# Weight loads of the first expert pairs issued at other points, and the last tile's row store in two halves

## The chip, the cores and the metric

The kernel runs on one core of a Trainium2 chip. The metric is the device time of one execution in microseconds (us). TensorE (PE) multiplies matrices, VectorE (DVE), ScalarE (ACT) and GpSimd (POOL) work elementwise, and SyncE (SP) does little but issue DMA transfers. Each engine takes its instructions strictly in the order in which they stand in the program, and waits on semaphores where they depend on another engine or on a transfer.

## The reference

One transformer layer over 1024 tokens of width 1024: a hybrid mixer (two kinds of gated linear attention, chunks of 16), a layer norm, and a mixture of experts with 64 experts of which each token takes two, then a second layer norm. What matters here is the second half:

```python
x = layer_norm(ALPHA * x + hybrid_mixer(x, ...), ln1_g, ln1_b)
# hierarchical_moe: the best of 8 groups, then the best two of its 8 experts, with gates
h = jax.nn.silu(xb_ @ w_gate[e]) * (xb_ @ w_up[e])     # per expert: 1024 -> 512
y = h @ w_down[e]                                      # 512 -> 1024, added to each token by its gate
x = layer_norm(ALPHA * x + y, ln2_g, ln2_b)
```

All 64 experts have three float32 matrices of 2 MB each, 384 MB in all, which are read once.

## The kernel before

**Stages.** Up to about 400 us the mixer runs. From there to about 535 us the output projection, the first norm and the router run over eight tiles of 128 tokens; each tile's normed rows go to the DRAM tensor `x1d` (`scaled_rows`, a store issued by ACT), and the router's counts become tables that say which tokens each expert gets. From about 535 us on the experts run in 32 pairs; a pair does two experts at once, each with up to 64 tokens in one half of the array. The first rows come from `x1d` by gathers (indirect DMAs that POOL issues by index tables); from pair 2 on PE picks a pair's rows out of a group of four pairs' rows (`picked`).

**Weights.** A weight matrix is a *unit* of 2 MB. Pair p owns units 6p to 6p+5: two gate matrices, two up matrices, two down matrices. PE multiplies all gate rows of a pair (`rows_by(p, 0, ...)`), then all up rows (`rows_by(p, 2, ...)`), then, after ACT's silu, DVE's product `sg` (silu(gate) times up), four PE transposes and DVE's copy `hT`, the down rows (`down`). Units wait in *rooms*: four `w1u`, four `w2u`, and for some early units two `w3u` rooms and a room in an old tile `VO1`. `load_unit(i)` issues unit i's load on SP's queue; `load_after(i)` issues the load that takes the room of unit i, after the product that read unit i. So the loads stand in one line on SP, and each waits until PE has freed its room. Units 4 to 10 are loaded during the router's last tiles: unit 9 in two halves, where the second half and unit 5 wait until the first gather has landed. Unit 11 takes the room of unit 0, unit 12 that of unit 1, 13 that of 2, 17 and 18 those of 8 and 9, 21 that of 12, 36 and 37 those of 28 and 29 (pair 4's down matrices), 38 and 39 those of 30 and 31 (pair 5's gate matrices).

**Order.** PE's order is the written one (`manual_schedule`). On the other engines a scheduler orders the instructions by its own estimate of when each can start, within the dependences; `after` and `order` in the code add further ones. In pair 4 DVE also spreads the second norm's vectors over partitions (`spread_out_rows`, a STREAM_SHUFFLE for each), applies the first norm's gain to gathered rows (`gained`) and finishes the first group's output rows (`finish_rows`).

Of the kernel before, what the change touches and what calls it, by code (L numbers as in the profile page):

```python
# [10 lines left out]
F32 = mybir.dt.float32  # L11
# [10 lines left out]
NT = T // 128  # L22
KT = D // 128
# [7 lines left out]
NOV = 80  # L31
# [28 lines left out]
def mixer_moe_kernel(ctx: ExitStack, tc: tile.TileContext, x_in, xT_in, wf_in, wv_in, wvg_in, wa2_in,  # L60
# [767 lines left out]
    sp2 = b1.enter_context(tc.tile_pool(name="sp2", bufs=2, reuse_waits="tile"))  # L828
    wr = rp.tile([128, KT, 72], F32, name="wr", bufs=1)
    S.dma_start(wr, wr_in)  # L830
    w1p = ctx.enter_context(tc.tile_pool(name="w1", bufs=W1N, side="right", reuse_waits="tile"))

    preR = tc.alloc_tile_pool(name="preR", bufs=1, side="right", reuse_waits="tile")
    rows = preR.tile([128, 4, 2, 512], F32, name="w3u")
# [5 lines left out]
    NU = 6 * npair  # L840
    utile = {}

    def load_unit(i):

        if i >= NU:
            return None
        src, e = units[i]
        shape = [128, 4, D] if src is wd_in else [128, KT, FF]
        r = i if i < 4 else (i - 2) if i < 10 else (i - 3 - (i > 19)) % (W1N + W2N)
        pool, name = ((preR if i == 4 else preL, "w3u") if i in (4, 5) else (voap, "VO1") if i in (10, 19) else  # L850
                      (w1p, "w1u") if r < W1N else (w2p, "w2u"))
        t = pool.tile(shape, F32, name=name)
        sv = src[e].rearrange("(p c) n -> p c n", c=4 if src is wd_in else KT)
        utile[i] = t
        if i == 9:
            pend.append((t[:, KT // 2:], sv[:, KT // 2:]))
            return nc.sync.dma_start(t[:, 0:KT // 2], sv[:, 0:KT // 2])
        if i < NU - NSPL:
            return nc.sync.dma_start(t, sv)
        if i % 2 == 0:  # L860
            pend.append((t, sv))
            return None
        cuts = (0, 1, 2, 3) if i == NU - 1 else (0, 4, 6, KT) if i == NU - 3 else (0, 2, 4) if src is wd_in else (0, 4, KT)
        both = pend[-1], (t, sv)
        for a_, b_ in zip(cuts, cuts[1:]):
            for t_, s_ in both:
                d = nc.sync.dma_start(t_[:, a_:b_], s_[:, a_:b_])
        for n in range(2) if i == NU - 1 else ():
            for t_, s_ in both:
                ns = slice(n * 512, (n + 1) * 512)  # L870
                d = nc.sync.dma_start(t_[:, 3, ns], s_[:, 3, ns])
        return d

    def load_after(i):

        if i not in (4, 5, 19):
            load_unit(i + W1N + W2N + (3 if i < 4 else 1 if i < 19 else 0))

    pend = []
    NSPL = 12  # L880
# [8 lines left out]
    def router(t):  # L889

        lt = lgt.pop(t)
        el = lt[:, 8:72].rearrange("p (g e) -> p g e", g=8)
        tl = lambda n, w, d=F32: sp2.tile([128, w], d, name=n)
        gm, gi = tl("gm", 8), tl("gi", 8, mybir.dt.uint32)
        V.max(gm, lt[:, 0:8])
        V.max_index(gi, gm, lt[:, 0:8])

        og = tl("og", 8)
        V.tensor_tensor(og, cst[:, C_I8:C_I8 + 8], gi[:, 0:1].to_broadcast([128, 8]), OP.not_equal)
        sel = sp2.tile([128, 8, 8], F32, name="sel")  # L900
        V.scalar_tensor_tensor(sel, og[:, :, None].to_broadcast([128, 8, 8]), -3e38, el, op0=OP.mult, op1=OP.add)
        sl = sel.rearrange("p g e -> p (g e)")
        em, ei = tl("em", 8), tl("ei", 8, mybir.dt.uint32)
        V.max(em, sl)
        V.max_index(ei, em, sl)
        rtop[t] = V.tensor_tensor(oh12[:, :, t], expert[:, None, :].to_broadcast([128, 2, NE]),
                                  ei[:, 0:2, None].to_broadcast([128, 2, NE]), OP.is_equal)
        m = sp2.tile([128, NE], BF, name="m", bufs=3)
        msb = sp2.tile([128, NE], BF, name="msb", bufs=3)
        V.tensor_copy(msb, msum)  # L910
        mop = V.tensor_tensor(m, oh1[:, t], oh2[:, t], OP.add)
        count = lambda: V.tensor_tensor(msum, msum, m, OP.add)

        fin = tl("fin", 1)
        order(V.tensor_tensor(fin, ei[:, 1:2], ei[:, 0:1], OP.is_gt), mop, "the ranks' product goes first")
        enc = sp2.tile([128, 2], F32, name="enc", bufs=3)
        V.scalar_tensor_tensor(enc, big2, fin, cst[:, C_TOK:C_I8].rearrange("p (a t) -> p a t", a=2)[:, :, t],
                               op0=OP.mult, op1=OP.add)
        mt[t] = m, msb, enc

        def gates(behind=None):

            gs = tl("gs", 8)
            gz = tl("gz", 1)
            ops = []
            V.tensor_scalar(gs, lt[:, 0:8], gm[:, 0:1], None, op0=OP.subtract)
            S.activation(gs, gs, AF.Exp, accum_out=gz)
            e2 = tl("e2", 1)
            S.activation(e2, em[:, 0:1], AF.Exp, bias=em[:, 1:2], scale=-1.0)
            gd = tl("gd", 1)  # L930
            ops.append(V.scalar_tensor_tensor(gd, e2, 1.0, gz, op0=OP.add, op1=OP.mult))
            V.reciprocal(gatev[:, t, 0:1], gd)
            V.tensor_tensor(gatev[:, t, 1:2], gatev[:, t, 0:1], e2, OP.mult)
            ops.append(count())
            if behind:
                for o in ops:
                    order(o, behind, "the rows that are to be fetched go first")

        if t < NT - 1:
            gates()  # L940
            return None
        return gates
# [105 lines left out]
    def scaled_rows(t):  # L1048

        r = rt[t]  # L1050
        rs, nm, _ = stats[t]
        for n in range(2):
            S.activation(r[:, n], r[:, n], AF.Identity, bias=nm, scale=rs)
        S.dma_start(x1d[t * 128:(t + 1) * 128].rearrange("p (a n) -> p a n", a=2), r)

    def logits(t):

# [386 lines left out]

    ys, outs, sums, ends, trow, grow = {}, [], {}, {}, [], []
    first = gather(xgs[2], sidx[:, 0:1])
    G.memset(one1, 1.0)
    G.memset(xgs[1], 0.0)
    for ld in (load_unit(5), nc.sync.dma_start(*pend.pop())):
        after(ld, first, "the rows of the first pair go before weights that are needed later")  # L1450

    def load_vectors():

# [15 lines left out]
    def pairs():  # L1469
# [4 lines left out]
        def rows_by(p, u, dst, xt, between={}):  # L1474
            for c in range(KT):
                for b in range(2):
                    PE.matmul(dst[64 * b:64 * b + 64], xt[:, c, 64 * b:64 * b + 64], utile[6 * p + u + b][:, c],  # L1477
                              start=(c == 0), stop=(c == KT - 1))
                if c in between:
                    between[c]()  # L1480
            for b in range(2):
                load_after(6 * p + u + b)

        def gate(p, gp):
            sg = mw.tile([128, FF], F32, name="sg", bufs=1)
# [16 lines left out]
        gather(xgs[0], sidx[:, 1:2])  # L1502
        fetch_rows(0, (1,))
        gp = ps_g.tile([128, FF], F32, name="gu")
        rows_by(0, 0, gp, xt)
        sg, _ = gate(0, gp)
        xt1 = transposed(xgs[0], xgs[2])
        up = ps_g.tile([128, FF], F32, name="gu")
# [141 lines left out]


    def block_tables():
        bt = w1p.tile([128, 4096], F32, name="w1u")
        at = [0]

        def t1(w):
# [115 lines left out]

    nfl = nc.values_load(over[0:1, 0:1], min_val=0, max_val=1, skip_runtime_bounds_check_because="a maximum of compares")  # L1773
    with tc.For_i(0, nfl):
        ovt = w1p.tile([128, 4, NOV], F32, name="w1u")
        ogate, oyid, oxid, oexp = ovt[:, 0], ovt[:, 1].bitcast(I32), ovt[:, 2].bitcast(I32), ovt[:, 3].bitcast(I32)
        block_tables()
        nblk = nc.values_load(onum[0:1, 0:1], min_val=0, max_val=NOV,
# [61 lines left out]
```

## Time and profile before

| | us |
|---|---|
| median of three runs | 1483.46 (1483.22 to 1483.67) |
| the profiled execution, its own time | 1484.21 |
| its span in the profile | 1482.4 |
| PE busy in the span | 1405.7 (95%) |
| DVE / ACT / POOL busy | 604.5 / 483.6 / 229.3 |
| bytes moved by DMA | 445.62 MB, mean 301 GB/s |

Each row of a timeline is a start, a duration, an engine, a source line, an operation with what it writes and reads, and in square brackets the engine's idle time before it and what ended it. Equal rows in sequence are merged (x2). "SPq" and "ACTq" are the queues of SP and ACT where a DMA is issued; a row of the DMA view gives the issues in a stretch of time, the size of one and the median time from issue to landing. The windows view gives for a stretch its length, the busy time of PE, PE's weight loads, DVE, ACT and POOL (number of instructions in brackets), the granted PE clock, the busy share of the 16 DMA engines and GB/s.

### The profile page before, as it was taken

To read this page: it belongs to the slowest core of one execution; us is meant where nothing else is said; L and a number is where in the kernel's file an instruction comes from. 1 tells how busy PE (TensorE), PEld (TensorE's weight loads), DVE (VectorE), ACT (ScalarE), POOL (GpSimd) and SP (SyncE) were. 2 spreads that over 40 slices of the span, in tenths; PEclk is the share of its full clock that TensorE was granted. 3 is DMA by queue.
4 is the path that set the end of the run, shared out by engine and by line. 5 is a ranking of instruction groups with operands and counts; after the bars stand their busy time and mean duration, and the time that the engine had idled before them with its cause. 6 is when DMAs were issued, how large, how long until landed. Compare 5 with 4: busy or idle time off the path is not lost. (4 is left out here: it accounts for less than half of the span.)

```text
span 1482.4 us, 25290 instructions
## 1 busy us (share of the span) xinstructions
PE 1405.7 (95%) x10651; PEld 822.1 (55%) x10651; DVE 604.5 (41%) x1465; ACT 483.6 (33%) x973; POOL 229.3 (15%) x165
## 2 busy tenths in 40 slices
PE   8999999999999989999998999998999998999996
PEld 7989889898888854344343344343433333433432
DVE  7577674867545843162141123133123013212313
ACT  6475555474413433312222211321222221221120
POOL 0000001010012212342402210130130130131000
PEclk9999999999999999999999999999999999999999
DMA  6110010101384479999999999999999999999995
GB/s 215 30 44 30 31 44 30 46 30 31 107 339 172 171 305 411 418 414 425 427 427 426 427 427 424 428 427 427 425 428 427 426 426 428 425 428 427 423 420 208
DMA packets 52944, 445.62 MB, mean 301 GB/s; under 512 B 9577, under 2 KB 10857, under 8 KB 27349
## 3 DMA queue, kind: packets, MB, share of 16 engines
q1 hardware_dynamic: 46344, 430.09, 70.2%
q0 software_dynamic: 4896, 8.84, 1.6%
q10 hardware_dynamic: 1584, 5.01, 0.9%
q8 instruction: 85, 1.39, 0.4%
q14 instruction: 35, 0.28, 0.1%
HBM read 440.33 MB, written 12.60 MB: 306 GB/s over the span
## 5 line engine op out<-in xcount | busy, mean ns | idle before, releaser
L1477 PE MATMUL gu<-w1u,VO 128*64 128x512 f32 x1040 | 252.5, 609 | 24.6 <-DMA w1u<-in_wu_dram 20.6
L1477 PE MATMUL gu<-w2u,VO 128*64 128x512 f32 x960 | 236.3, 607 | 23.0 <-DMA w2u<-in_wu_dram 22.7
L1230 ACT ACTIVATE VO<-tp,cols 128x128 f32<-128x128 f32 x256 | 96.1, 457 | 308.7 <-PE tp L1242 300.3
L1602 DVE TENSOR_TENSOR sg<-sg,gu 128x512 f32<-128x512 f32 x30 | 20.6, 688 | 420.3 <-PE gu L1477 420.3
L1477 PEld LDWEIGHTS gu<-w1u,VO 128*64 128x64 f32 x1040 | 80.0, 140 | 184.8 <-issue 142.7
L1477 PEld LDWEIGHTS gu<-w2u,VO 128*64 128x64 f32 x960 | 80.2, 140 | 167.6 <-issue 130.9
L1466 PE MATMUL gu<-w1u,hT 128*64 128x512 f32 x496 | 117.1, 598 | 2.0 <-issue 1.8
L176 PE MATMUL pp<-xh,wl 128*128 128x512 f32 x288 | 113.1, 393 | 0.0
L176 PE MATMUL pp<-xl,wh 128*128 128x512 f32 x288 | 113.0, 392 | 0.0
L176 PE MATMUL pp<-xh,wh 128*128 128x512 f32 x288 | 113.0, 392 | 0.0
L1466 PE MATMUL gu<-w2u,hT 128*64 128x512 f32 x480 | 109.5, 598 | 0.0
L1281 DVE SCALAR_TENSOR_TENSOR y<-gu,gcol,y 128x512 fp32r<-128x512 f32 x60 | 44.8, 749 | 141.1 <-ACT y L1280 141.0
L1242 PEld LDWEIGHTS <-parts 128*128 128x128 bf16 x1248 | 69.9, 98 | 46.9 <-issue 46.8
L1280 ACT ACTIVATE y<-gu,gcol 128x512 fp32r<-128x512 f32 x60 | 41.1, 686 | 158.3 <-PE gu L1466 157.9
L1486 ACT ACTIVATE sg<-gu 128x512 f32<-128x512 f32 x31 | 18.5, 597 | 188.9 <-PE gu L1477 188.9
L1242 PE MATMUL tp<-pick,parts 128*128 128x128 bf16 x1248 | 80.1, 220 | 0.0
L1466 PEld LDWEIGHTS gu<-w1u,hT 128*64 128x64 f32 x496 | 35.5, 136 | 59.8 <-issue 55.4
L1466 PEld LDWEIGHTS gu<-w2u,hT 128*64 128x64 f32 x480 | 32.7, 136 | 62.3 <-issue 61.5
L176 PEld LDWEIGHTS pp<-xh,wl 128*128 128x128 f32 x288 | 54.1, 188 | 11.5 <-issue 0.5
L176 PEld LDWEIGHTS pp<-xl,wh 128*128 128x128 f32 x288 | 54.1, 188 | 11.2 <-issue 0.2
L176 PEld LDWEIGHTS pp<-xh,wh 128*128 128x128 f32 x288 | 54.1, 188 | 11.0
L1395 POOL TENSOR_TENSOR rest<-VO,parts 128x1024 f32<-128x1024 f32 x11 | 29.7, 2698 | 194.2 <-ACT parts L1392 129.9
(401 smaller groups left out, 2209.2 us busy)
## 6 DMA issues: line engine op xcount, KB each, us to landing
w1u<-in_wg_dram SPq DMA_DIRECT2D x30, 2048.0 KB, 27.8
w2u<-in_wu_dram SPq DMA_DIRECT2D x30, 2048.0 KB, 27.9
w1u<-in_wu_dram SPq DMA_DIRECT2D x29, 2048.0 KB, 29.9
w2u<-in_wg_dram SPq DMA_DIRECT2D x29, 2048.0 KB, 25.8
w1u<-in_wd_dram SPq DMA_DIRECT2D x29, 2048.0 KB, 29.9
w2u<-in_wd_dram SPq DMA_DIRECT2D x28, 2048.0 KB, 29.0
wr<-in_wf_dram SPq DMA_DIRECT2D x36, 256.0 KB, 2.7
w1u<-in_wu_dram SPq DMA_DIRECT2D x6, 1024.0 KB, 23.5
```

What stands on the lines that cost most here:

```text
L176: PE.matmul(ps, w[:, k], x_[:, k, ts], start=(k == j == 0), stop=(k == KT - 1 and j == 2))
L1230: S.activation(xt[:, c], tp[:, i], AF.Identity, bias=cols[:, 42 + c:43 + c], scale=cols[:, 34 + c:35 + c])
L1242: PE.matmul(o, part[:, c], m, start=(i == 0), stop=(i == len(ms) - 1))
L1280: S.mul(yh[:, ns], yps[n], gate_col)
L1281: return V.scalar_tensor_tensor(yl[:, ns], yps[n], gate_col, yh[:, ns], op0=OP.mult, op1=OP.subtract)
L1395: first = E.tensor_tensor(rest, x, b0, OP.subtract)
L1466: PE.matmul(yps[n][64 * b:64 * b + 64], hT[:, c, 64 * b:64 * b + 64], utile[6 * p + 4 + b][:, c, n * 512:(n + 1) * 512], start=(c == 0), s ...
L1477: PE.matmul(dst[64 * b:64 * b + 64], xt[:, c, 64 * b:64 * b + 64], utile[6 * p + u + b][:, c], start=(c == 0), stop=(c == KT - 1))
L1486: return sg, S.activation(sg, gp, AF.Silu)
L1602: V.tensor_tensor(sg, sg, up, OP.mult)
```

## The change

1. Unit 9 loads whole where its first half was issued.
2. Unit 5 waits for a small POOL instruction (`one1`'s memset) that now stands behind the first gather's issue, not for the gather's landing.
3. Units 11 and 12 write into the tiles of units 0 and 1 themselves (a reshaped view, so that dependences are kept by parts of the tile) and load in two halves each: the first half after half of pair 0's gate product, the second at its end. For that the four `w1u` rooms become four tiles of their own names.
4. The last token tile's rows are stored to `x1d` in two halves, each after its own ACT pass.
5. The last tile's small cast `msb` (128x64) moves from DVE to ACT.

```diff
-    w1p = ctx.enter_context(tc.tile_pool(name="w1", bufs=W1N, side="right", reuse_waits="tile"))
+    w1p = ctx.enter_context(tc.tile_pool(name="w1", bufs=1, side="right", reuse_waits="tile"))
...
-    def load_unit(i):
+    def load_unit(i, half=None):
...
-                      (w1p, "w1u") if r < W1N else (w2p, "w2u"))
-        t = pool.tile(shape, F32, name=name)
-        sv = src[e].rearrange("(p c) n -> p c n", c=4 if src is wd_in else KT)
+                      (w1p, f"w1u{r}") if r < W1N else (w2p, "w2u"))
+        n = shape[1]
+        if i in (11, 12):
+            t = utile[i - 11].rearrange("p a b -> p (a b)").rearrange("p (a b) -> p a b", a=n)
+        else:
+            t = pool.tile(shape, F32, name=name)
+        sv = src[e].rearrange("(p c) n -> p c n", c=n)
+        if half is not None:
+            utile[i] = t
+            cs = slice(half * n // 2, (half + 1) * n // 2)
+            return nc.sync.dma_start(t[:, cs], sv[:, cs])
         utile[i] = t
-        if i == 9:
-            pend.append((t[:, KT // 2:], sv[:, KT // 2:]))
-            return nc.sync.dma_start(t[:, 0:KT // 2], sv[:, 0:KT // 2])
...
-        V.tensor_copy(msb, msum)
+        (S.copy if t == NT - 1 else V.tensor_copy)(msb, msum)
...
+        dst = x1d[t * 128:(t + 1) * 128].rearrange("p (a n) -> p a n", a=2)
         for n in range(2):
             S.activation(r[:, n], r[:, n], AF.Identity, bias=nm, scale=rs)
-        S.dma_start(x1d[t * 128:(t + 1) * 128].rearrange("p (a n) -> p a n", a=2), r)
+            if t == NT - 1:
+                S.dma_start(dst[:, n], r[:, n])
+        if t < NT - 1:
+            S.dma_start(dst, r)
...
     first = gather(xgs[2], sidx[:, 0:1])
-    G.memset(one1, 1.0)
+    issued = G.memset(one1, 1.0)
     G.memset(xgs[1], 0.0)
-    for ld in (load_unit(5), nc.sync.dma_start(*pend.pop())):
-        after(ld, first, "the rows of the first pair go before weights that are needed later")
+    order(issued, first, "the rows of the first pair go before weights that are needed later")
+    after(load_unit(5), issued, "the rows of the first pair go before weights that are needed later")
...
             for b in range(2):
-                load_after(6 * p + u + b)
+                load_after(6 * p + u + b, None if p or u else 1)
...
-        rows_by(0, 0, gp, xt)
+        rows_by(0, 0, gp, xt, {KT // 2 - 1: lambda: [load_after(b, 0) for b in range(2)]})
```

**SP's loads around the first gather.** The rows are units 8, 9 (first half), 5, 9 (second half), 11, 12, 13 before, and 8, 9, 5, then the halves of 11 and 12, and 13 with the change. DMASW0 is the first gather's landing; PE is a wait for a room.

```order
L859 DMA w2u_6557<-in_wu_dram 128x4096 [waits PE_49]
L857 DMA w2u_6559<-in_wu_dram 128x2048 [waits DVE_49,PE_49]
L859 DMA w3u_6684<-in_wd_dram 128x4096 [waits DVE_49,DMASW0_49,PE_49,DMAHW0_49,Activation_49,Pool_49]
L1449 DMA w2u_6559<-in_wu_dram 128x2048 [waits DMAHW1_49]
L859 DMA w1u_6745<-in_wd_dram 128x4096 [waits DMAHW2_49,PE_49]
L859 DMA w1u_6747<-in_wg_dram 128x4096 [waits DMAHW3_49,PE_49]
L859 DMA w1u_6797<-in_wg_dram 128x4096 [waits DMAHW4_49,PE_49]
```

With the change the same place on SP reads:

```order
L864 DMA w2u_6557<-in_wu_dram 128x4096 [waits PE_49]
L864 DMA w2u_6559<-in_wu_dram 128x4096 [waits DVE_49,PE_49]
L864 DMA w3u_6685<-in_wd_dram 128x4096 [waits DVE_49,PE_49,DMAHW1_49,Activation_49,Pool_49]
L861 DMA w1u0_5306<-in_wd_dram 128x2048 [waits DMAHW2_49,PE_49]
L861 DMA w1u1_5308<-in_wg_dram 128x2048 [waits DMAHW3_49,PE_49]
L861 DMA w1u0_5306<-in_wd_dram 128x2048 [waits DMAHW4_49,PE_49]
L861 DMA w1u1_5308<-in_wg_dram 128x2048 [waits DMAHW5_49,PE_49]
L864 DMA w1u2_6797<-in_wg_dram 128x4096 [waits DMAHW6_49,PE_49]
```

The wait for the gather's landing is gone from unit 5, unit 9 is one transfer, and four half loads stand where units 11 and 12 stood.

**DVE in pair 4.** `sg_7365` is pair 4's product of silu(gate) and up, and waits for the last matmul of pair 4's up product; `hT_7456` is the copy behind it, for which the down product waits. The shuffles spread the norm's vectors, `cp_6988` and `cp_6989` are sums of the first group. Before:

```order
L1281 SCALAR_TENSOR_TENSOR y_7283<-gu_7282,gcol_5108,y_7283 128x512
L1462 STREAM_SHUFFLE VO1_7213<-VO1_7213 128x1024 x2
L1326 TENSOR_TENSOR VO0_65<-VO0_65,VO1_7213 128x1024
L1462 STREAM_SHUFFLE VO1_7213<-VO1_7213 128x1024
L1327 TENSOR_TENSOR VO0_65<-VO0_65,VO1_7213 128x1024
L1462 STREAM_SHUFFLE VO1_7213<-VO1_7213 128x1024
L1439 SCALAR_TENSOR_TENSOR VO0_65<-VO0_65,cp_6988 128x512
L1439 SCALAR_TENSOR_TENSOR VO0_65<-VO0_65,cp_6989 128x512
L1440 BN_STATS st_7375<-VO0_65 128x6 x2
L1602 TENSOR_TENSOR sg_7365<-sg_7365,gu_7344 128x512
```

With the change:

```order
L1290 SCALAR_TENSOR_TENSOR y_7283<-gu_7282,gcol_5108,y_7283 128x512
L1611 TENSOR_TENSOR sg_7365<-sg_7365,gu_7344 128x512
L1471 STREAM_SHUFFLE VO1_7213<-VO1_7213 128x1024 x2
L1335 TENSOR_TENSOR VO0_65<-VO0_65,VO1_7213 128x1024
L1471 STREAM_SHUFFLE VO1_7213<-VO1_7213 128x1024
L1336 TENSOR_TENSOR VO0_65<-VO0_65,VO1_7213 128x1024
L1471 STREAM_SHUFFLE VO1_7213<-VO1_7213 128x1024
L1448 SCALAR_TENSOR_TENSOR VO0_65<-VO0_65,cp_6988 128x512
L1448 SCALAR_TENSOR_TENSOR VO0_65<-VO0_65,cp_6989 128x512
L1449 BN_STATS st_7375<-VO0_65 128x6 x2
L1269 COPY hT_7456<-tp_7451 128x512
```

`sg_7365` moved from behind the nine norm instructions to ahead of them; `hT_7456` stays behind them. No line of the diff touches this place: the scheduler placed it anew. Behind it the first two output tiles' small norm steps are interleaved otherwise, with the same instructions; elsewhere DVE's order differs by the moved cast alone.

**ACT at the last tile.** Its rows before, with `x1d_66` the stored rows:

```order
L1068 COPY xt_6539<-xtp_6528 128x512 [waits PE_49]
L1068 COPY xt_6545<-xtp_6533 128x512 [waits PE_49]
L1053 ACTIVATE VO0_65<-VO0_65,nm1_6511,rs1_6510 128x512 [waits DMAHW1_49,DVE_49]
L1053 ACTIVATE VO0_65<-VO0_65,nm1_6511,rs1_6510 128x512
L927 ACTIVATE gs_6620,gz_6621<-gs_6620 128x8 [waits DVE_49]
L1054 DMA x1d_66<-VO0_65 128x1024 [waits DMAHW7_49,Activation_49]
```

With the change:

```order
L915 CAST msb_6579<-msum_5093 128x64 [waits DVE_49]
L1077 COPY xt_6539<-xtp_6528 128x512 [waits PE_49]
L1077 COPY xt_6545<-xtp_6533 128x512 [waits PE_49]
L1059 ACTIVATE VO0_65<-VO0_65,nm1_6511,rs1_6510 128x512 [waits DMAHW1_49,DVE_49]
L1059 ACTIVATE VO0_65<-VO0_65,nm1_6511,rs1_6510 128x512
L1061 DMA x1d_66<-VO0_65 128x512 [waits DMAHW7_49,Activation_49]
L1061 DMA x1d_66<-VO0_65 128x512 [waits DMAHW0_49,Activation_49]
L932 ACTIVATE gs_6621,gz_6622<-gs_6621 128x8 [waits DVE_49]
```

The cast came in ahead of the two copies, and two stores of half the size stand where one stood, ahead of the small exponential.

More of the change, by code (lines that the diff above doesn't have):

```diff
@@ L872, in load_unit, with load_after @@
         return d
-    def load_after(i):
+    def load_after(i, half=None):
         if i not in (4, 5, 19):
-            load_unit(i + W1N + W2N + (3 if i < 4 else 1 if i < 19 else 0))
+            load_unit(i + W1N + W2N + (3 if i < 4 else 1 if i < 19 else 0), half)
     pend = []
@@ L1652, in block_tables @@
     def block_tables():
-        bt = w1p.tile([128, 4096], F32, name="w1u")
+        bt = w1p.tile([128, 4096], F32, name="w1u0")
         at = [0]
@@ L1774, in mixer_moe_kernel @@
     with tc.For_i(0, nfl):
-        ovt = w1p.tile([128, 4, NOV], F32, name="w1u")
+        ovt = w1p.tile([128, 4, NOV], F32, name="w1u1")
         ogate, oyid, oxid, oexp = ovt[:, 0], ovt[:, 1].bitcast(I32), ovt[:, 2].bitcast(I32), ovt[:, 3].bitcast(I32)
```

## The prediction

> **What bounds the kernel now.** I read the costliest groups first, then windows over the expert stage, then PE's timeline for its first wait on a weight load.
>
> ```profile
> L1477 PE MATMUL gu<-w1u,VO 128*64 128x512 f32 x1040 | 252.5, 609 | 24.6 <-DMA w1u<-in_wu_dram 20.6
> L1477 PE MATMUL gu<-w2u,VO 128*64 128x512 f32 x960 | 236.3, 607 | 23.0 <-DMA w2u<-in_wu_dram 22.7
> 700.00:1400.00 700.00, 651.74 (x3531) 273.75 (x3529) 174.23 (x407) 155.61 (x295) 135.27 (x70) 0.98 1.01 427
> 761.64 7.08 PE L1477 MATMUL gu<-w2u,VO 128*64 128x512 f32 x30 [0.93 <-DMA w2u<-in_wu_dram]
> ```
>
> PE is busy 95% of the span, yet the end is set by the transfers: the gate and up matmuls stand idle 24.6 + 23.0 us, nearly all of it for weight loads, and from 700 to 1400 us the DMA engines are full (share 1.01, 427 GB/s). PE waits for a load for the first time at 761.64. So a microsecond gained or lost in the line of loads counts at the end only if that line never stands still later; a microsecond of PE counts only where it delays a room. A unit of 2 MB at 427 GB/s takes 4.9 us.
>
> Before 700 the line does stand still:
>
> ```profile
> 576.00:580.00 4.00, 3.34 (x16) 1.18 (x12) 2.27 (x4) 1.71 (x3) 3.22 (x1) 1.00 0.92 328
> 600.00:604.00 4.00, 4.00 (x20) 1.29 (x18) 0.00 (x0) 2.50 (x2) 1.36 (x1) 1.00 0.88 320
> 577.80 0.33 SPq L859 DMA_DIRECT2D w2u<-in_wd_dram  x1
> 588.05 12.19 SPq L859 DMA_DIRECT2D w1u<-in_wu_dram  x2
> ```
>
> At 578 and at 601 the rate falls to 328 and 320 GB/s: the queue has run dry, because unit 17 (issued 577.80) and unit 21 (the second of the pair of issues from 588.05 to 600.24) wait until PE has freed their rooms. After these two points the line is as early as PE's products let it be, whatever it had loaded ahead.
>
> **The loads: no gain.** These are the loads that the change moves:
>
> ```profile
> 521.00 0.33 SPq L859 DMA_DIRECT2D w2u<-in_wu_dram  x1
> 523.74 0.33 SPq L857 DMA_DIRECT2D w2u<-in_wu_dram  x1
> 538.25 0.33 SPq L859 DMA_DIRECT2D w3u<-in_wd_dram  x1
> w2u<-in_wu_dram SPq DMA_DIRECT2D x1, 2048.0 KB, 7.8
> ```
>
> Unit 9's second half (1 MB, 2.45 us of the line) goes out at 523.74 and no longer behind the gather. Unit 5 goes out behind the gather's issue, near 536.1 and not 538.25, 2.2 us earlier. Together the line is 2.45 + 2.2, about 4.6 us ahead when pair 0 begins. The halves of units 11 and 12 can start half a gate product earlier (3.5 of the 7.09 us below), 2 MB that also goes out ahead. All of it is lost at 578 and 601, where the rooms of units 17 and 21 come free by PE's pace: the queue will only run dry sooner and longer. I count 0. Were it carried to the end it would be −4.6 (first rival). The two more issues on SP cost 0.33 us each while SP waits for rooms: 0, and 0.7 if that cover were gone.
>
> **The last store and the first gather: +1.3.**
>
> ```profile
> 524.65 0.39 DVE L910 CAST msb<-msum 128x64 bf16<-128x64 f32 x1
> 524.96 0.68 DVE L1019 BATCH_NORM_STATS2 st<-VO 128x6 f32<-128x512 f32 x1
> 524.72 0.59 ACT L1068 COPY xt<-xtp 128x512 f32<-128x512 f32 x1 [3.01 <-PE xtp L1063]
> 528.25 1.52 ACT L1053 ACTIVATE VO<-VO,nm,rs 128x512 f32<-128x512 f32 x2 [2.19 <-DVE rs L1044]
> 529.80 0.33 ACTq L1054 DMA_DIRECT2D x1d<-VO  x1
> x1d<-VO ACTq DMA_DIRECT2D x1, 512.0 KB, 3.9
> x1d<-VO ACTq DMA_DIRECT2D x1, 512.0 KB, 5.4
> 534.63 1.21 POOL L1213 DMA_INDIRECT VO<-x1d,sidx  x1 [9.64 <-DVE rhs L1182]
> 535.31 2.96 PE L1500 MATMUL tp<-cst 128*128 128x128 f32 x14 [0.29 <-DVE gcol L1187]
> 538.16 1.16 PE L1236 MATMUL tp<-cst,VO 128*128 128x128 f32 x8
> VO<-x1d,gidx POOLq DMA_INDIRECT x1, 10.0
> ```
>
> The cast leaves DVE, so the last tile's norm statistics can start up to 524.96 − 524.65 = 0.31 us earlier; ACT, idle 3.01 us there, takes the cast for nothing. I take 0.2, since the chain to `rs` also goes through other engines. ACT's two passes then end near 529.55, and the store's second half goes out at 529.6 (the first at 528.9). In the run of before the store issued at 529.80 landed 3.9 us later, at 533.7, and the first gather started 0.9 us behind that, at 534.63. But there only half of unit 9 lay in the engines beside it; now it is all of it. The nearest row with a whole unit beside the store is the second store above (tile 4's, issued at 508.82, unit 10 having been issued at 504.28): 5.4 us. 529.6 + 5.4 = 535.0, 1.3 later than 533.7. Ends: −0.2 if the additional megabyte does not touch the store, and 529.6 + 3.9 + 2.45 = 535.95, +2.25, if the store waits for all of it. I take +1.3, by the row that has the same neighbours. The gather then starts near 535.9, and pair 0's rows reach PE near 539.5 and not 538.16; everything behind it moves along, the releases of units 17 and 21 too, so this term stays to the end.
>
> [...]
>
> [...] The first gather took 538.16 − 534.63, at most 3.5 us, and unit 5 issued 1.5 us into it needs time to start; I take 0. The other end is the third gather, issued among loads: 10.0 us, +6.4 (third rival). The 14 idle transposes at 535.31 keep their place.
>
> **DVE's order in pair 4: +4.4.** This is the largest term and is in none of the edits: the product `sg` of pair 4, which waits for PE's up product, now stands ahead of the norm instructions.
>
> ```profile
> 646.07 0.75 DVE L1281 SCALAR_TENSOR_TENSOR y<-gu,gcol,y 128x512 fp32r<-128x512 f32 x1 [3.92 <-ACT y L1280]
> 645.11 13.90 PE L1477 MATMUL gu<-w2u,VO 128*64 128x512 f32 x64
> 646.75 1.34 DVE L1462 STREAM_SHUFFLE VO<-VO 128x1024 f32<-128x1024 f32 x1
> 657.30 1.27 DVE L1440 BATCH_NORM_STATS2 st<-VO 128x6 f32<-128x512 f32 x2
> 659.15 0.69 DVE L1602 TENSOR_TENSOR sg<-sg,gu 128x512 f32<-128x512 f32 x1 [0.58 <-PE gu L1477]
> 662.89 0.68 DVE L1260 COPY hT<-tp 128x512 f32<-128x512 f32 x1
> 663.67 3.65 PE L1466 MATMUL gu<-w1u,hT 128*64 128x512 f32 x16 [1.76 <-issue]
> 673.72 0.48 DVE L1372 TENSOR_SCALAR own<-place,places 128x128 f32<-128x128 bf16 x2
> 674.37 7.09 PE L1477 MATMUL gu<-w1u,VO 128*64 128x512 f32 x32
> 646.75:659.15 12.40, 12.40 (x62) 4.09 (x59) 11.82 (x15) 0.60 (x1) 10.98 (x4) 1.00 0.99 416
> 659.15:674.40 15.25, 12.76 (x98) 7.14 (x95) 15.04 (x38) 4.67 (x11) 7.79 (x4) 1.00 1.01 429
> ```
>
> Before, DVE fills the 12.4 us of PE's up product with 11.82 us of norm work, from 646.75 to 658.57, and `sg` follows at once at 659.15. With the change DVE stands at `sg` from 646.8 to 659.15, ends it at 659.84, and then has the 11.82 us ahead of `hT`: `hT` starts at 671.66 and not 662.89. PE's down product starts 8.77 later, at 672.44. Behind it DVE has no room to catch up (15.04 us busy of 15.25 up to 674.40), so the second `own`, from which PE picks pair 5's rows, ends 11.8 later, at 686.0, and pair 5's gate product starts near 686.2.
>
> PE then stands idle some 10 us before the down product, and that costs clock as well:
>
> ```profile
> 532.00:536.00 4.00, 1.97 (x19) 1.71 (x20) 2.40 (x18) 0.00 (x0) 1.21 (x1) 0.50 0.03 10
> 536.00:540.00 4.00, 3.90 (x25) 3.29 (x25) 0.31 (x3) 1.09 (x4) 1.99 (x2) 0.77 0.54 133
> ```
>
> After the idle time around 530 PE was granted half its clock. In 536 to 540 the mean is 0.77, which is 1.84 us at half; with the 0.7 us from 535.31 to 536 that is some 2.5 us at half speed, a loss of 1.3 us.
>
> PE has slack for such a delay, the line of loads has less. What it costs is read at the rooms that pair 4's down product and pair 5's gate product free:
>
> ```profile
> 672.38 0.81 SPq L859 DMA_DIRECT2D w1u<-in_wg_dram  x2
> 681.48 0.80 SPq L859 DMA_DIRECT2D w1u<-in_wu_dram  x2
> w1u<-in_wg_dram SPq DMA_DIRECT2D x2, 2048.0 KB, 18.3
> w1u<-in_wu_dram SPq DMA_DIRECT2D x1, 2048.0 KB, 15.2
> ```
>
> Units 36 and 37 were issued at 672.38 and 672.85 and landed one unit apart; the second took 18.3 us, so the first landed at 672.85 + 18.3 − 4.9 = 686.3. With the change they go out at 672.4 + 8.8 + 1.3 = 682.5 into a queue that has emptied, where a unit lands 7.8 us after its issue (unit 8): 690.3, +4.0. Units 38 and 39: before, 681.48 + 15.2 = 696.7; with the change 681.48 + 11.8 + 7.8 = 701.1, **+4.4**. That is the larger one and decides. Ends: 2.7 if the clock does not fall and only units 36 and 37 count (681.2 + 7.8 = 689.0); 5.7 if pair 5's gate also runs into half clock (4.4 + 1.3). After 700 the DMA engines never rest, so this stays to the end.
>
> **Sum.** On the profiled execution, 1484.21 (0.75 above the median of the runs): 1484.21 + 0 + 1.3 + 4.4 = 1489.9; against the median of 1483.46, 1489.2. With the terms' ends, 2.5 to 8.0, the main case reaches from 1486.0 to 1491.5.
>
> **Rivals.** First, the lead carries: the loads 4.6 us ahead keep it past 578 and 601, and the delay in pair 4 stays hidden behind it, so 1483.5 − 4.6 = 1478.8, faster. It decides if units 17 and 21 find their rooms free when SP reaches them; the two dry windows speak against it. Chance 0.04.
>
> Second, no loss from DVE's order. The line before has 15.2 to 18.3 us from issue to landing against 7.8 in an empty queue, 7 to 10 us of cover against a delay of 9 to 12; if `hT`'s delay came out under 7 us, or the loads found other slack before 761.64, only the store's term is left: 1483.3 to 1484.8, no change. For it: PE's first wait for a load comes 80 us later. Against: share 1.01 from 659 to 674 and from 700 on, so a gap there isn't made good. Chance 0.15.
>
> Third, the first gather is caught by unit 5's packets: 10.0 instead of 3.5 us, +6.4 on top of the main case, 1495.6. For it: no wait keeps them apart now. Against: the 1.5 us between. Chance 0.06.
>
> **Numbers.** Main case 0.73, the three rivals 0.04, 0.15 and 0.06, 0.02 for others. A measurement of this kernel tells some 0.2%, 3 us, from no change. Faster than 1480.5: 0.05. Within: the second rival and the main case's lower tail, 0.18. Slower than 1486.4: 0.77. The range goes from 1484.5 (part of the second rival) to 1492.5.
>
> **What would show it.** DVE's row of `sg` near 660 followed by the shuffles, `hT` near 673 (the 671.7 moved by the +1.3), PE idle about 10 us before pair 4's down product, pair 5's gate near 687, and a hole in the DMA share between 680 and 697. The last store landing 5.4 us after its issue, the first gather near 535.9, unit 5 about 1.5 us behind it. The dry windows near 578 and 601 still there. It is wrong if these two have vanished (first rival), if the DMA share keeps to 1.01 between 680 and 697 (second), or if pair 0's first transposes wait beyond 541 (third).

## The result, and the profile after

The changed kernel takes 1496.32 us (median of four runs, 1496.2 to 1497.62) where the kernel before takes 1483.57 (1483.22 to 1486.46). The ratio is 1.0084, 95% interval 1.0071 to 1.0098: 12.5 us slower, between 10.5 and 14.5. The forecast was 5.7. The profiled execution has a span of 1494.6 us, 12.2 more than before.

The groups of costliest instructions and PE's first wait for a weight load show the same limit as before: the loads. PE's waits for them did not become longer (25.4 and 21.6 us, before 24.6 and 23.0). PE first waits for a load at 824 and not at 762, because it is itself later.

```profile
L1486 PE MATMUL gu<-w1u,VO 128*64 128x512 f32 x1040 | 249.6, 608 | 25.4 <-DMA w1u<-in_wu_dram 23.1
L1486 PE MATMUL gu<-w2u,VO 128*64 128x512 f32 x960 | 236.3, 608 | 21.6 <-DMA w2u<-in_wu_dram 21.5
824.12 7.09 PE L1486 MATMUL gu<-w1u,VO 128*64 128x512 f32 x32 [0.41 <-DMA w1u<-in_wg_dram]
```

**Start of the expert stage.** These rows of the timeline, with one of the DMA view and two windows, show the last store, the first gather and pair 0 in the changed kernel:

```profile
x1d<-VO ACTq DMA_DIRECT2D x1, 256.0 KB, 6.5
536.91 1.21 POOL L1222 DMA_INDIRECT VO<-x1d,sidx  x1 [12.03 <-DMA x1d<-VO]
VO<-x1d,sidx POOLq DMA_INDIRECT x1, 3.6
538.27 0.33 SPq L864 DMA_DIRECT2D w3u<-in_wd_dram  x1
540.57 1.16 PE L1245 MATMUL tp<-cst,VO 128*128 128x128 f32 x8 [2.33 <-DMA VO<-x1d,sidx]
541.84 8.78 PE L1486 MATMUL gu<-w1u,VO 128*64 128x512 f32 x32
...
540.00:544.00 4.00, 3.33 (x14) 1.66 (x16) 0.00 (x0) 2.67 (x8) 0.72 (x1) 0.77 0.91 374
544.00:548.00 4.00, 4.00 (x18) 1.33 (x16) 0.00 (x0) 0.22 (x1) 0.00 (x0) 0.80 0.56 226
```

The store's second half was issued at 529.5 and landed 6.5 us later, at 536.0. The gather waited for it and started at 536.91, 2.28 us later than before. (The row of before names a DVE instruction as the gather's releaser, but there too the gather started 0.9 us behind the store's landing.) PE stood idle 2.33 us, then worked from 541.84 at a mean clock of 0.77 to 0.80, so that pair 0's gate took 8.78 us instead of 7.09. In all unit 18's load was issued 4.1 us later, at 582.34 instead of 578.24.

**Pair 4.** DVE, PE and SP's issues, and the windows over the same time:

```profile
663.26 0.69 DVE L1611 TENSOR_TENSOR sg<-sg,gu 128x512 f32<-128x512 f32 x1 [12.33 <-PE gu L1486]
663.87 1.33 DVE L1471 STREAM_SHUFFLE VO<-VO 128x1024 f32<-128x1024 f32 x1
675.53 0.69 DVE L1269 COPY hT<-tp 128x512 f32<-128x512 f32 x1
676.32 6.52 PE L1475 MATMUL gu<-w1u,hT 128*64 128x512 f32 x16 [10.31 <-issue]
687.90 0.82 SPq L864 DMA_DIRECT2D w1u<-in_wg_dram  x2
690.15 7.09 PE L1486 MATMUL gu<-w1u,VO 128*64 128x512 f32 x32
697.26 0.80 SPq L864 DMA_DIRECT2D w1u<-in_wu_dram  x2
...
w1u<-in_wg_dram SPq DMA_DIRECT2D x1, 2048.0 KB, 8.1
w1u<-in_wu_dram SPq DMA_DIRECT2D x1, 2048.0 KB, 9.9
...
676.00:680.00 4.00, 3.68 (x10) 1.36 (x12) 4.00 (x8) 0.00 (x0) 3.92 (x3) 0.50 1.00 426
680.00:684.00 4.00, 4.00 (x31) 1.79 (x28) 4.00 (x15) 0.69 (x1) 2.14 (x1) 0.73 0.18 74
684.00:688.00 4.00, 4.00 (x23) 1.37 (x21) 3.93 (x11) 1.56 (x5) 1.05 (x1) 1.00 0.00 0
```

DVE waits 12.33 us for PE's up product, then does `sg`, the shuffles and the norm, and reaches `hT` at 675.53. PE is idle 10.31 us and runs the first half of the down product at half clock (0.50 from 676 to 680; 6.52 instead of 3.65 us). The DMA engines run empty from 681 to 688 (share 0.02). Units 36 and 37 are issued at 687.90 instead of 672.38; unit 38 is issued at 697.26 and lands at 707.2 (before: 696.7), 10.5 us later.

From there to the end 1.7 us are added. The last issues of weights, before and with the change:

```profile
1455.74 4.94 SPq L871 DMA_DIRECT2D w1u<-in_wd_dram  x4
1467.96 4.92 SPq L876 DMA_DIRECT2D w1u<-in_wd_dram  x4
```

The line of loads ends 12.2 us later, the whole of the span's difference. The landing of unit 38 and this last row are the two marks by which the experiments are read below.

### The profile page after: what moved, and what is told of

Read it like the earlier page. It is cut to its first block, busy times and chain, and to the rows that moved or that the text cites. A ratio compares the mean times of both kernels' runs of the same rounds, so it can differ in the third digit from the quotient of the medians.

```text
span 1494.6 us, 25296 instructions
## 1 busy us (share of the span) xinstructions
PE 1407.8 (94%) x10651; PEld 824.0 (55%) x10651; DVE 604.3 (40%) x1464; ACT 483.5 (32%) x974; POOL 228.3 (15%) x165
## 5 line engine op out<-in xcount | busy, mean ns | idle before, releaser
L1486 PE MATMUL gu<-w1u,VO 128*64 128x512 f32 x1040 | 249.6, 608 | 25.4 <-DMA w1u<-in_wu_dram 23.1
L1486 PE MATMUL gu<-w2u,VO 128*64 128x512 f32 x960 | 236.3, 608 | 21.6 <-DMA w2u<-in_wu_dram 21.5
## 6 DMA issues: line engine op xcount, KB each, us to landing
w2u<-in_wg_dram SPq DMA_DIRECT2D x29, 2048.0 KB, 24.6
```

## Experiments

Each experiment is timed against the kernel before on the same chip, which there had medians of 1484.4 (e1 to e4), 1484.3 (e5, e7 to e9) and 1485.7 (e6, e10). Where no interval stands, the time is that of a single run, and the kernel is read by its trace alone. The marks:

| kernel | unit 38 lands | last weights issued | time against before, us |
|---|---|---|---|
| before | 696.7 | 1455.7 | |
| the change | 707.2 | 1468.0 | +12.5 (10.5 to 14.5) |
| e1, DVE's order back | 699.6 | 1459.5 | +4.0 (2.4 to 5.6) |
| e2, DVE's order alone | 704.7 | 1465.4 | +10.2 (8.3 to 12.2) |
| e3, the change, one gap filled in part | 707.2 | 1469.0 | +13.8 (11.7 to 15.7) |
| e4, e1 and unit 9 in halves | 696.3 | 1456.8 | −0.1 (−1.5 to 1.2) |
| e5, e1, clock held at the start | 698.2 | 1458.3 | +2.4, single run |
| e6, e1, the last store whole | 700.1 | 1460.8 | +5.0, single run |
| e7, e2, both gaps filled | 701.9 | 1469.4 | +13.5 (11.1 to 15.7) |
| e8, e4 with three quarters of unit 9 | 696.8 | 1456.5 | +0.6, single run |
| e9, e4 with a warm start | 694.9 | 1455.7 | −0.1 (−1.5 to 1.2) |
| e10, e7 with a cast moved | 702.8 | 1464.4 | +6.8 (4.5 to 9.4) |

### Two causes apart: e1 and e2

e1 is the changed kernel with DVE's order in pair 4 as before:

```diff
-            V.tensor_tensor(sg, sg, up, OP.mult)
+            gated = V.tensor_tensor(sg, sg, up, OP.mult)
+            if p == 4:
+                order(gated, ends["stats"], "the norm's sums go first")
```

> The changed kernel with DVE's order in pair 4 as it was before (sg behind the nine norm instructions, by one added ordering); all five edits stay. Theory now: two costs add up. The first gather starts 2.28 us later (536.91 against 534.63), pair 0's gate product takes 8.78 instead of 7.09 us at a granted clock near 0.8, and the unit loads from 578 on are issued 4.1 us later (582.34 against 578.24); the rest of the 12.2 us of the span, some 8, comes from DVE's order. So here +4.1 over before, 1487.6. Rival one, everything from DVE's order: 1483.5. Rival two, the late start is partly taken up by the line of loads (one unit issued at 663.14 landed only 1.8 us later than its counterpart): +1.8, 1485.3.

e2 is the kernel before with only that order changed:

```diff
-                spread_out_rows(ln1)
+                norm = spread_out_rows(ln1)
...
-                spread_out_rows(ln2)
+                norm += spread_out_rows(ln2)
...
+            if p == 4:
+                for o in norm:
+                    order(o, gated, "the gate goes first")
...
+            if p == 4:
+                order(ends["turn"], ends["stats"], "the norm's sums go first")
```

> The kernel before with only DVE's order in pair 4 changed to that of the changed kernel (sg first, then the nine norm instructions, then hT). Theory: +8.1, 1491.6: pair 4's down product starts 8.8 us later and runs its first half at half clock (6.5 instead of 3.65 us), pair 5's gate 11.7 us later, and the DMA engines stand empty for some 6 us near 680. My prediction's term: +4.4, 1487.9. Rival, the start costs little and the order nearly all: +10 or more, 1493.5.

e1 came out 4.0 us slower than before and e2 10.2. By the marks unit 38 is late by 2.9 in e1 and 8.05 in e2, together 10.95 against 10.5 in the change; at the last weights 3.8 and 9.6, together 13.4 against 12.2. The two costs add up within 1.2 us, and neither rival of e1 (all from DVE, or most of the start taken up) holds. The order alone costs about twice the 4.4 of the prediction. At unit 38 e2 is late by what I had expected of its time (8.1); in time it came out at its rival's figure (+10 or more), though not for the rival's reason, since e1 shows that the start is not cheap. Some 1.5 us are added behind unit 38, and their cause is open.

### The start: e4, e8, e6, e5

e4 is e1 with unit 9 in halves, the second half and unit 5 behind the gather's issue:

```diff
+        if i == 9:
+            pend.append((t[:, KT // 2:], sv[:, KT // 2:]))
+            return nc.sync.dma_start(t[:, 0:KT // 2], sv[:, 0:KT // 2])
...
-    after(load_unit(5), issued, "the rows of the first pair go before weights that are needed later")
+    for ld in (load_unit(5), nc.sync.dma_start(*pend.pop())):
+        after(ld, issued, "the rows of the first pair go before weights that are needed later")
```

> e1 with unit 9 in two halves again; its second half and unit 5 both go out behind the first gather's issue and not its landing. Theory: the whole of unit 9 beside the last store is what made the gather late. The store lands near 533.5, the gather starts near 534.3, pair 0's gate takes 7.1 us, and the time is that of before, 1483.2 to 1483.5, although unit 5, unit 9's second half and the halves of 11 and 12 still go out earlier: their lead is worth nothing. Rival one, the two stores of half the size are what is late (6.6 us each for a half of the bytes): still +4.1, 1487.6. Rival two, unit 5 behind the gather's issue slows that gather: pair 0 starts 2 us or more later than 538.2. Rival three, the lead is worth something: below 1482.

e8 is e4 with the cut at three quarters:

```diff
-            pend.append((t[:, KT // 2:], sv[:, KT // 2:]))
-            return nc.sync.dma_start(t[:, 0:KT // 2], sv[:, 0:KT // 2])
+            pend.append((t[:, 6:], sv[:, 6:]))
+            return nc.sync.dma_start(t[:, 0:6], sv[:, 0:6])
```

> e4 with unit 9 split at three quarters: 1.5 MB ahead of the last store, 0.5 MB behind the gather. The second half store landed 4.0 us after its issue with half of unit 9 ahead of it (e4), 7.2 with the whole (e1). Theory: the store lands when the bytes ahead of it have drained, so 0.5 MB more is 1.2 us more: 5.2 us, and the gather starts about 1 us later than the tables allow. [...]

e6 is e1 with the store in one piece:

```diff
         for n in range(2):
             S.activation(r[:, n], r[:, n], AF.Identity, bias=nm, scale=rs)
-            if t == NT - 1:
-                S.dma_start(dst[:, n], r[:, n])
-        if t < NT - 1:
-            S.dma_start(dst, r)
+        S.dma_start(dst, r)
```

> e1 with the last tile's rows stored by one transfer again, unit 9 whole. Theory: the store lands when unit 9 ahead of it has drained, whatever its cut: near 536.5, as the two halves did, and the first gather starts near 537. Rival: two transfers of 256 KB, each spread over all DMA engines, are what is slow: then the gather starts a microsecond or more earlier.

The DMA view's row of the store and the first gather in the timeline, for e4, then e8, then e6:

```profile
x1d<-VO ACTq DMA_DIRECT2D x2, 256.0 KB, 4.0
535.03 1.21 POOL L1225 DMA_INDIRECT VO<-x1d,sidx  x1 [9.44 <-DVE rhs L1194]
```

```profile
x1d<-VO ACTq DMA_DIRECT2D x2, 256.0 KB, 5.5
535.85 1.21 POOL L1225 DMA_INDIRECT VO<-x1d,sidx  x1 [10.95 <-DVE omsb L1326]
```

```profile
x1d<-VO ACTq DMA_DIRECT2D x1, 512.0 KB, 6.6
536.91 1.22 POOL L1219 DMA_INDIRECT VO<-x1d,sidx  x1 [12.11 <-DMA x1d<-VO]
```

With 1, 1.5 and 2 MB of unit 9 ahead of it the store takes 4.0, 5.5 and 6.5 to 7.2 us, whether it is cut (6.5 in the change, 7.2 in e1) or whole (6.6 in e6). Each half megabyte costs 1.0 to 1.7 us, about what it takes to move (1.2 at 427 GB/s). The 5.5 us of e8 lie between the 5.2 that I had expected of a store that waits for the bytes ahead of it and the 5.6 halfway between 4.0 and 7.2, for one that they only slow in proportion, so that time does not decide between the two; the landings and the queues do. In the change unit 9 landed at 534.9 and the store's second half 1.1 us behind it; in e1, e6 and the kernel before the store landed 1.2, 0.9 and 1.3 us behind unit 9. These are rows of the changed kernel's queues from 531 to 532, then 533 to 534, then 534 to 535 (packets, MB, share of the 16 engines); q1 is SP's, q10 carries ACT's stores:

```profile
q1 hardware_dynamic: 18, 0.29, 109.7%
q10 hardware_dynamic: 95, 0.19, 48.0%
q10 hardware_dynamic: 170, 0.30, 78.5%
```

Up to 532 none of the store's packets had moved, 2.5 us after its second half's issue. So in these four runs the store's landing followed that of unit 9, 0.9 to 1.3 us behind it. The two stores of half the size neither help nor hurt (6.5 and 7.2 us against 6.6 for the whole). With unit 9 in halves the time is that of before, and the gather with unit 5 issued behind it took 4.1 us in e4 and 3.6 in the change, so that the second rival of e4 did not come. The upper end of the prediction's term for the store (+2.25), where it waits for the whole of unit 9, is what came (+2.28).

e5 is e1 with more idle transposes ahead of pair 0:

```diff
-        for i in range(14):
+        for i in range(28):
             PE.transpose(idle[:, i % 4], ident, ident)
```

> e1 with 28 instead of 14 idle transposes ahead of pair 0. In e1 PE stood idle 3.01 us for the late gather and then ran the first rows' transposes in 1.86 and pair 0's gate in 8.00 us (1.16 and 7.09 before). Theory: that is clock, lost to the wait; with the gap filled the transposes take 1.16 to 1.8 and the gate 7.09, and the loads from 578 on go out about 1 us earlier than in e1, counted from the gather. Rival: the gate is slow because unit 9's and 5's packets or the halves stand in its way: still 8 or more.

```profile
535.18 5.99 PE L1509 MATMUL tp<-cst 128*128 128x128 f32 x28 [0.29 <-DVE gcol L1196]
541.38 1.16 PE L1245 MATMUL tp<-cst,VO 128*128 128x128 f32 x8 [0.22 <-DMA VO<-x1d,sidx]
542.64 7.09 PE L1486 MATMUL gu<-w1u,VO 128*64 128x512 f32 x32
```

PE's timeline of e5 has the first rows' transposes at 1.16 and the gate at 7.09 us again, where e1 had 1.86 and 8.00 and the change 1.16 and 8.78. Unit 38 lands at 698.2 and not at 699.6. The time, of a single run, is 1.6 us below e1's. So the start costs through two things: a gather that waits, and PE's clock, which falls behind that wait (to 0.50 from 542.18 to 545.59 in the change).

### The lead of the early loads: e9

e9 is e4 with 18 idle transposes in PE's gaps ahead of the gather (10 behind the tables of the seventh tile, 3 and 5 around the first half of the last tile's):

```diff
+    def warmed(n, behind=None):
+        for i in range(n):
+            w = PE.transpose(warm[:, i % 4], ident, ident)
+            if behind:
+                order(w, behind, "the clock is kept")
+            behind = w
+        return w
+    up0 = warmed(10, tb_last[0])
     ranks(t)
-    table_part(0, tabp[:, 0:32])
+    order(ends_pe[0], up0, "the clock is kept")
+    up1 = warmed(3, ends_pe[0])
+    order(table_part(0, tabp[:, 0:32]), up1, "the clock is kept")
+    up2 = warmed(5, tp_last[0])
...
-    table_part(1, gt)
+    order(table_part(1, gt), up2, "the clock is kept")
```

> e4 with 18 more idle transposes on PE in its gaps between 528.7 and 534.8, ahead of the first gather, so that the clock is up when the first rows come. In e4 the first rows' transposes took 1.77 instead of 1.16 us and the line of loads was issued 1.4 to 1.7 us later than before (579.96 against 578.24), and yet the unit issued at 601.75 landed at 613.85, 0.8 earlier than its counterpart before: the lead of the early loads does count there by some 2 us, against my prediction, and the late start hides it. Theory: with the clock up, transposes 1.16, units issued 0.6 to 1.4 us earlier than in e4, the line 1 to 2 us ahead of before at 615 and to the end: 1482.5 to 1483.5 where before stands at 1484.4. Rival: the lead is worth nothing, 1484.4. Rival two: the transposes delay the tables, the gather starts later than 535.3.

Here pair 0 runs at full clock at the time of before (transposes at 538.28, gate at 539.55 in 7.09 us). Unit 22 is issued at 600.45, 0.1 later than before, and lands at 612.55 and not at 614.64; unit 38 lands 1.8 us earlier than before. So the lead is worth some 2 us there, not nothing. The line before had not run dry at 601: unit 22 took 14.3 us from its issue to its landing there and 12.1 in e9, where the engines had emptied further at the first of the two points (0.70 of 576 to 580, before 0.92). But the last weights are issued at 1455.7 as before, and the time is the same within 1.5 us, not the 1 to 2 us better that I had expected. Where the 1.8 us went between 697 and 1455 the traces do not show; that stays open. The distance between the two marks differs from kernel to kernel, from 759.1 us (before) to 761.8 (e3) among the kernels other than e7, which has a stop in between.

### The order: e3, e7, e10

e3 is the changed kernel with PE kept busy in pair 4's gap:

```diff
             if p == 4:
                 finish_rows(0, 1)
+                idle = ps_x.tile([128, 4, 128], F32, name="tp")
+                for i in range(60):
+                    PE.transpose(idle[:, i % 4], ident, ident)
...
```

In e3, and in e7 and e10 below, one more ordering, not printed here, keeps DVE's last scaled rows of pair 4 behind `own`.

> The changed kernel with 60 idle transposes on PE in pair 4, between the last of the first group's sums and the down product, where PE stood idle 10.3 us; nothing waits for them but PE. Theory: half clock is 2.9 us of the order's cost. PE keeps its clock, the down product's first half takes 3.65 instead of 6.52 us, the two loads issued at 687.90 go out near 685.0, and the next two, whose issue hangs on pair 5's gate, stay near 697.3: the line lands 2.1 us earlier there, 1494.2. Rival, the clock does not matter because the later pair of loads decides, as the prediction had it: 1496.3, no change.

e7 is e2 with both of PE's gaps filled, pair 4's as in e3 but with 86 transposes, and the one ahead of the last small product for the next group's rows with 20:

```diff
+            if g == 2 and q == 2:
+                idle = ps_x.tile([128, 4, 128], F32, name="tp")
+                for i in range(20):
+                    PE.transpose(idle[:, i % 4], ident, ident)
             PE.matmul(tp, m, tokf[:, col], start=(q == 0), stop=(q == GP - 2))
```

> e2 (before with DVE's changed order alone) and idle transposes on PE in its two gaps: 86 ahead of pair 4's down product (idle 10.31 us in e2) and 20 ahead of the last small product for pair 5's rows (idle 2.46 us). DVE's order and its delay stay. Theory: the clock is what the prediction's term lacked. Down product's first half 3.65 instead of 5.07 us, pair 5's gate 7.09 instead of 10.01 us, the two loads of pair 4's rooms issued near 681.3 and those of pair 5's near 693.4 (696.33 in e2), landing near 701.5 (704.73): the cost falls from some 9 to the 4.4 to 5 that I had predicted, 1489. Rival, the loads' lateness has another cause than the clock: as e2, 1493.5.

PE's timeline in e2, e3 and e7, from pair 4's down product (x16) to pair 5's gate (x32):

```profile
672.25 5.07 PE L1465 MATMUL gu<-w1u,hT 128*64 128x512 f32 x16 [10.31 <-issue]
685.77 0.58 PE L1373 MATMUL tp<-tokf,own 128*128 128x1 f32 x2 [2.46 <-DVE own L1372]
686.29 10.01 PE L1476 MATMUL gu<-w1u,VO 128*64 128x512 f32 x32
```

```profile
676.08 5.35 PE L1475 MATMUL gu<-w1u,hT 128*64 128x512 f32 x16 [3.36 <-DVE hT L1269]
689.67 0.38 PE L1382 MATMUL tp<-tokf,own 128*128 128x1 f32 x2 [2.24 <-DVE own L1381]
689.99 8.78 PE L1486 MATMUL gu<-w1u,VO 128*64 128x512 f32 x32
```

```profile
672.40 3.65 PE L1469 MATMUL gu<-w1u,hT 128*64 128x512 f32 x16 [0.56 <-DVE hT L1260]
685.97 0.38 PE L1377 MATMUL tp<-tokf,own 128*128 128x1 f32 x2 [1.39 <-DVE own L1372]
686.28 7.09 PE L1480 MATMUL gu<-w1u,VO 128*64 128x512 f32 x32
```

In e2 a gap of 10.31 us costs 1.42 us of the down product, and a gap of 2.46 us costs 2.92 us of pair 5's gate. In e3 the 60 transposes were done early, in some 7 us (estimated from the two gaps, 10.31 − 3.36), so that a gap of 3.36 us was left; the down product took 5.35 us and not the 3.65 expected, 1.2 less than in the change, but the gap ahead of pair 5's gate grew from 1.00 to 2.24 us and cost 1.69. Unit 38 landed where it did in the change and the time did not fall: my expectation (−2.1) was wrong, since I had left the second gap's clock out. The rival's figure, no change, came: units 36 and 37 went out 1.4 us earlier than in the change, but unit 38, which waits for pair 5's gate, 1.5 us later (698.80 against 697.26). In e7 both gaps are filled, both products run at full clock, units 36 and 38 are issued at 681.11 and 693.40 and unit 38 lands at 701.9, all as expected up to there. The clock thus makes 2.8 of the 8.05 us at this mark, the delay in DVE 5.2.

And yet e7 is slower than e2, 13.5 us over before where I had expected some 5. The stop is further on, in pair 6. These rows are POOL's two gathers of the next group's rows in e2, then the same two in e7 with ACT, PE and a window:

```profile
696.18 1.03 POOL L1213 DMA_INDIRECT VO<-x1d,gidx  x1 [0.30 <-issue]
697.95 1.00 POOL L1213 DMA_INDIRECT VO<-x1d,gidx  x1 [0.73 <-DMA out_dram<-VO,gidx]
```

```profile
705.62 1.03 POOL L1213 DMA_INDIRECT VO<-x1d,gidx  x1 [10.21 <-DMA out_dram<-VO,gidx]
706.96 1.00 POOL L1213 DMA_INDIRECT VO<-x1d,gidx  x1 [0.31 <-issue]
722.43 2.02 ACT L1396 CAST parts<-VO 128x1024 bf16<-128x1024 f32 x1 [14.07 <-DMA VO<-x1d,gidx]
724.87 13.02 PE L1480 MATMUL gu<-w1u,VO 128*64 128x512 f32 x48 [8.77 <-ACT VO L1230]
720.00:740.00 20.00, 15.02 (x67) 5.68 (x68) 1.88 (x3) 6.89 (x12) 4.74 (x2) 0.75 0.74 296
```

One of the two gathers may start only when the second scatter of output rows has left its room; the other need not wait for that. In e2 the free one stands first, right behind the issue of the second scatter. In e7 the scheduler placed them the other way round, though no line of the edit touches POOL: the first stands 10.21 us at the scatter, and the free one, whose rows ACT's cast needs, stands behind it. It landed at 722.4, the cast stood 14.07 us on ACT, and PE waited for ACT's copies behind the cast. The slow scatters alone do not make the stop: in e3, where both took 11 us as in e7 but the gathers stand as in e2, the cast waits 1.94 us. So e7's time holds a cost that e2 and the change do not have, and e7 tells of the clock's price at unit 38 alone. e10 has POOL's order of e7 and moves that cast behind the silu of pair 6:

```diff
-            if p > 2 and q > 1 and g + 1 < NG:
+            if p > 2 and q > 1 and g + 1 < NG and p != 6:
                 split_rows(g + 1, q - 2, G)
...
+            if p == 6:
+                split_rows(g + 1, 0, G, behind=silu)
```

> e7 with one move on ACT: in pair 6 the cast of the next group's first gathered rows (at which ACT stood 14.07 us in e7, with PE idle 8.77 us behind it and the DMA engines at 0.74 of 720 to 740) is ordered behind that pair's silu. All else as e7, idle transposes included. Theory: e7's time is two costs, the loads' 5.2 us (units of pair 5's rooms land at 701.9 against 696.7) and the rows that come late behind the output scatters; without the second, PE does not stop at 716, the DMA share from 720 to 740 is 1.0 again and the time is some 5 over before, 1489 to 1490. Rival: the wait only moves to the next use of these rows, 1496 or more.

```profile
713.24 13.90 PE L1480 MATMUL gu<-w1u,VO 128*64 128x512 f32 x64
720.00:740.00 20.00, 19.89 (x108) 8.22 (x106) 5.41 (x8) 9.88 (x15) 7.79 (x3) 1.00 1.01 427
```

PE runs through, the DMA share is 1.01, and the time is 6.8 us over before, 4.5 to 9.4. That is above the 5 I expected, within the interval. e10 thus confirms that the stop at the cast is what made e7 slower than e2. Its 6.8 against the 10.2 of e2 leaves some 3.4 us in time for the clock, near the 2.8 at unit 38, though the two intervals overlap. No run has e7's transposes with POOL's order of e2.

## Why the prediction was wrong in size

The direction, the limit (the line of loads) and both places were right; the time lay outside the range because both terms were too small. The step that failed in both is the clock of PE behind a wait; in the first the store was also taken as too short.

- **Which part costs.** Both terms stood in the sum and both were found, at the instructions named: the first gather behind the store, and `sg` ahead of the norm.
- **The store and the first gather.** Forecast +1.3, measured +4.0 (e1). Two things failed. The size: I took the row of tile 4's store, 5.4 us, and the store behind the whole of unit 9 took 6.5; the gather came 2.28 later, my upper end. That row did not have the same neighbours: unit 10 landed 8.7 us after its issue, unit 9, which stood behind unit 8, 11.3 after its own. Tile 4's store landed 1.3 us behind unit 10, and that distance, not the 5.4 us, is what carries over. And a step was missing: in the sum pair 0 only moves along, but PE's 2.33 us of waiting brought half clock into pair 0's gate, 1.69 us more. Together that is nearly all of the 4.1 us by which unit 18's load is late. At unit 38 e1 is 2.9 late; that the lead of the loads took up the difference is argued from e9, not shown apart.
- **DVE's order.** Forecast +4.4, measured +8.05 at unit 38 and +10.2 in time (e2). The delays on DVE and PE are those of the sum: 8.6 to 8.8 us for the down product, 11.9 for pair 5's gate (686.29 against 674.37). What failed is the clock. I put 1.3 us on the down product alone, and let pair 5's gate run at full clock but for the range's end, with 1.3 again. The 4.4 is that of the loads behind pair 5's gate, so it has no clock in it, neither the 1.3 of the down product nor any of the gate. The runs show 1.42 and 2.92 in e2, 2.87 and 0 in the change. With the clock held the term is 5.2 at unit 38 (e7), of which 0.7 comes from a landing of 8.5 where I had 7.8.
- **The loads: no gain.** Right for the time (e4 and e9, −0.1 each), but not by the step given: the lead is not all lost at 578 and 601. I read the dips to 328 and 320 GB/s as a queue that had run dry, but the engines were still busy to 0.92 and 0.88. In e9 unit 22, issued at the same time as before, lands 2.1 us earlier, and the gain is gone only by the last weights. That the term came out at 0 is luck as far as is known.
- **The rivals.** The lead carried to the end is refuted by e4 and e9. No loss from DVE's order is refuted by e2 and by the DMA share of 0.00 from 684 to 688. The third one's time, 1495.6, is near the measured one, but its mechanism did not occur, so that is chance: the first gather landed 3.6 us after its start, with unit 5 issued 1.36 behind it.
- **The signs named.** `sg` followed by the shuffles, PE's idle 10 us and the hole in the DMA share came as described; the hole lay from 681 to 688, inside the stretch named, and went down to 0.00. The two dips of the line are there too, 4 us later. `hT` was at 675.5 (673 forecast), the gather at 536.91 (535.9).

## What to carry to other kernels

An edit of loads can move an instruction on an engine that it does not touch, by way of the scheduler; the larger part of this loss stands in the order of DVE's instructions and in no line of the diff. Which of the five edits moved it was not tried. An experiment can suffer the same: idle transposes on PE turned round two gathers on POOL (e7). Where a wait on PE is priced, price the clock behind it too, for each gap, also for a short one (2.24 us of idle time cost 1.69 in e3): here a third of the order's cost (2.8 of 8.05 us at unit 38) and nearly half of the start's (1.69 of the 4.1 by which unit 18's load is late). Where others wait for a small store behind a big load, cut the load so that the part ahead of the store is small (in e4 the store took 4.0 us behind half of unit 9, in the change 6.5 behind the whole).

## What the runs showed of the hardware

**In these runs the clock's price did not follow the length of the gap.** A gap of 10.31 us cost the product behind it 1.42 us in e2 and 2.87 in the change; gaps of 2.24, 2.33 and 2.46 us cost 1.69, 1.69 and 2.92; gaps of 1.00 (the change) and 1.39 (e7) cost nothing. What it followed is the stretch of half clock, of which these windows show two, in e2 and in the change:

```profile
664.92:675.14 10.22, 2.88 (x8) 1.11 (x10) 10.22 (x14) 0.00 (x0) 10.14 (x5) 0.50 1.00 428
668.48:682.12 13.64, 5.80 (x14) 1.92 (x16) 13.64 (x22) 0.00 (x0) 13.56 (x5) 0.50 0.90 382
```

In e2 half clock lasts until 675.15 and the down product starts at 672.25, so 2.90 us of work run at half speed, which costs half of that, 1.45 (1.42 measured). In the change it lasts until 682.13 and the product starts at 676.32: 5.81 us, 2.9 by the same sum (2.87 measured). The stretches of clock 0.50 that the windows show are 3.41 us long in the change behind the gap of 2.33 (542.18 to 545.59), 6.83 before around the first gather (531.01 to 537.84), 10.22 in e2 and 13.64 in the change, about one to four times the shortest of them. The loss can come late: in the change the transposes right behind the gap of 2.33 us still ran in 1.16 us, half clock began at 542.18, and the gate was slow.

**Indirect transfers of 0.5 MB took 10 us and more beside the loads, and 2.8 in the hole.** In the change the first output scatter, issued at 686.72 into the hole (DMA share 0.02 from 681 to 688), landed 2.8 us later, and the second, issued at 690.32 with the loads back (0.96 from 690 to 694), 10.8 later; in e7 both scatters, issued at 682.85 and 694.42, landed 10.8 and 10.9 us later.
